# Seven block products instead of eight in two of eight weight pieces, in half of u and in z, with the scan's decay in another buffer

## The chip, the cores and the metric

One NeuronCore of a Trainium2 chip runs one program. The metric is the device time of one execution in microseconds, from runs of the unchanged kernel and of the changed one; lower is better. The engines are named as the profile names them: PE is TensorE's matmul side, PEld its weight loads, DVE is VectorE, ACT is ScalarE, POOL is GpSimd, SP is SyncE, which here only issues the weights' transfers.

## The reference

One decoder layer over 256 tokens of width 2048, float32, batch 1. The part that matters here is the mixer between two feed-forward blocks:

```
proj = rmsnorm(h, mix_norm) @ w_in            # 2048 x 10272
gu, gv, z, xbc, dt_raw = split(proj)          # u, v, z: 2048 columns each
a_out = chunked_sgu(gelu(gu), gelu(gv), ...)  # u * (W_s RMSNorm(v) + b)
...
seg   = cum[:, :, :, None] - cum[:, :, None]
decay = exp(where(causal, seg, -inf))         # 128 x 128 for each of 32 heads, in 2 chunks
y_diag = einsum('bclsg,bclsgr,bcsgrp->bclgrp', scores, decay, xdt)
...
m_out = rmsnorm(y * silu(z), ssm_norm)
h = h + concat([a_out, m_out]) @ w_out
```

## The kernel before

**Products.** Every float32 operand is split into a high part and the rest (`hi`, `lo`), and a product of two is three matmuls: hi by hi, hi by lo, lo by hi. Weights stream in pieces of 256 rows by 1024 columns (1 MB); a piece is the block matrix of 2 row blocks by 2 column groups of 512. ACT writes `hi` (`high`, L161), DVE writes `lo` (`split_op`, L169). There are three buffers for `raw`, three for `hi` and two for `lo`, so `lo` of a piece is written when the last piece but one is done.

**Two ways through a piece.** With 256 tokens as 2 blocks of 128, a piece is 8 block products of 128 x 128 by 128 x 512, so 24 matmuls. `proj_tok` (L204) does that: its operands are transposed tokens, four accumulators of 512 columns. `proj_sum` (L245) knows two kinds of pieces. A piece "C" is done plainly, 24 matmuls. A piece "S" is done with 7 block products, 21 matmuls, after Strassen and Winograd: DVE forms four sums of the weight blocks (`split_sums`, L189), these are split too (`wshigh`, `wslow`, one buffer each), and the token operand holds sums as well (`Pieces.sums`, L415). Four of the seven products lie in accumulators of their own (m1, m6, m5, m7), from which ACT and DVE build parts (`parts_of`, L468), to which the plain accumulators are added at the end. The feed-forward blocks, `w_out`, the values and `w_o` use `proj_sum` already; V, u and z, two halves each, use `proj_tok`.

**The scan.** `scan_start(t, j)` (L750) handles 16 heads of chunk t: it brings a row of 2048 cumulative sums from DRAM to all 128 partitions (tile `dec`, 1 MB, issued by POOL), and for j = 0 makes `xdt` and y times D. DVE then makes three passes over `dec` (minus `cum`, minimum with `lim`, and, after ACT's exponential, times the scores). `scan_apply` (L774) uses `dec` as weights for 16 matmuls in two accumulators (`yp`), which DVE adds to y. `dec` is a tile of the pool `big`, which has 12 buffers of 8 KB per partition and holds the operands too.

**What sets the order.** PE runs in program order, written by hand: `step()` counts half pieces and pieces, and `later(fn, by)` puts side work (transposes, the scan) at a step. The scan's four starts stand at steps 3, 7, 13, 17 from the start of V and its four applications at 7, 10, 17, 21 (L826). On DVE, ACT and POOL a scheduler orders the instructions when the program is built, and each engine runs its own in that order; waits are semaphores. `split_op` keeps the splits among themselves in order.

Of the kernel before, what the change touches and what calls it, by code (L numbers as in the profile page):

```python
# [46 lines left out]
def hybrid_layer(ctx: ExitStack, tc: tile.TileContext, x, mem, w_gu1, w_dn1, w_in, w_s, w_out,  # L47
# [24 lines left out]
    def matmul(out, lhsT, rhs, start=False, stop=False):  # L72
        return pe(nc.tensor.matmul(out, lhsT=lhsT, rhs=rhs, start=start, stop=stop))  # L73
# [130 lines left out]
    def proj_tok(w, r0, xts, cs, evac, kts=D // P):  # L204

        n = kts // KP
        ps = {}
        for i in range(n):
            hi, lo = split(load(w, r0 + i * KP * P, cs, PLAIN))
            order = [(t, k) for k in range(KP) for t in range(NT)]  # L210
            if i in (0, n - 1):
                order.sort()
            for t, k in order:
                if t not in ps:
                    ps[t] = [side("acc") for _ in range(2)]
# [109 lines left out]
        junk = half_k(F32, "junk")  # L325
        return nc.scalar.activation(junk, src, AF.Square, accum_out=ss)

    def rstd_of(ss, name):
        n = ss.shape[1]
        r = small.tile([P, n], F32, name=f"rstd_{name}", bufs=1)  # L330
# [107 lines left out]
    class Normed:  # L438


        def __init__(self, name, c0, kinds=None):
            self.name, self.c0 = name, c0
            self.xts = [] if kinds is None else Pieces(kinds, f"xp_{name}")
            self.ss = small.tile([P, NT, 4], F32, name=f"ss_{name}", bufs=1)

        def chunk(self, n, by=1):
            srcs = [h[n][:, t, :] for t in range(NT)]
            if isinstance(self.xts, Pieces):

                for i in (2 * n, 2 * n + 1):  # L450
                    later(lambda i=i: self.xts.put(i, srcs, i % 2 * KP, self.c0 + n * KG),
                          {4: 1, 6: 1.5, 5: 2.5, 7: 3}.get(i, by))
                later(lambda: self.stats(n), 3)
            else:
                operand_later(srcs, self.xts, f"xt_{self.name}{n}", self.c0 + n * KG, by)
                self.stats(n)

        def stats(self, n):
            for t in range(NT):
                sum_sq(self.ss[:, t, n:n + 1], h[n][:, t, :])  # L460
            if n == 3:
                self.rstd = rstd_of(self.ss, self.name)

    def axpy(y, a, x):
        return nc.vector.scalar_tensor_tensor(out=y, in0=x, scalar=a, in1=y, op0=ALU.mult, op1=ALU.add)
# [46 lines left out]
    def ffn(nrm, w_gu, w_dn, done=None, each=None, fine=0):  # L515
        for c_from, c_to in ((0, 5), (5, 11)):
# [61 lines left out]
    nx = Normed("mix", C_MIX)  # L578
    ffn(n1, w_gu1, w_dn1, nx.chunk, fine=2)


# [51 lines left out]
    def raw_dts():  # L633


        wd = whigh.tile([P, 2 * KP, NC], F32R, name="hi").rearrange("p a n -> p (a n)")[:, :2 * NC]
        wd = wd.rearrange("p (k h) -> p k h", h=2 * HEADS)
        nc.scalar.copy(out=wd[:, :, :HEADS], in_=raw_dt)
        nc.vector.tensor_tensor(out=wd[:, :, HEADS:], in0=raw_dt, in1=wd[:, :, :HEADS].bitcast(F32), op=ALU.subtract)
        pdt = side("dt")  # L640
        for k in range(D // P):
            matmul(pdt[:2 * HEADS, :], wd[:, k, :], nx.xts[k // KG][:, k % KG, :],
                   start=(k == 0), stop=(k == D // P - 1))
# [106 lines left out]
    def scan_start(t, j):  # L750
        hs = slice(j * 16, j * 16 + 16)
        if j == 0:
            scan["xdt"] = scan[f"xdt{t}"] = xdt = slot([P, HEADS, HD], F32, "xdt")
            nc.vector.tensor_tensor(out=xdt, in0=y[t], in1=per_head(dt[:, t, :], HD), op=ALU.mult)
            nc.vector.tensor_tensor(out=y[t], in0=y[t], in1=per_head(rowb[:, 2, :], HD), op=ALU.mult)
        dec = slot([P, 16, P], F32, "dec")
        nc.gpsimd.dma_start(
            out=dec.rearrange("p h l -> p (h l)"),
            in_=cum_rows[t:t + 1, j * 16 * P:(j + 1) * 16 * P].broadcast_to([P, 16 * P]))
# [101 lines left out]
    for c in (0, 2):  # L861
        gss = [[], []]

        def evac(t, ps):
            for j in range(2):
                g = half_k(F32, "gate")
                nc.scalar.activation(g, ps[j], AF.Gelu_apprx_tanh, scale=rstd[:, t:t + 1])
                nc.vector.scalar_tensor_tensor(out=g, in0=v[t][:, c + j, :],
                                               scalar=col[:, C_GB + c + j:C_GB + c + j + 1],
                                               in1=g, op0=ALU.add, op1=ALU.mult)  # L870
                gss[j].append(g)

        proj_tok(w_in, 0, nx.xts, (U0 + c * NC, U0 + (c + 1) * NC), evac)
        for j in range(2):
            ats.later(gss[j], by=1 + j)

    ss_m = small.tile([P, NT, 4], F32, name="ss_m", bufs=1)
    for c in (0, 2):
        def evac(t, ps):
            for j in range(2):  # L880
                g = half_k(F32, "gate")
                nc.scalar.activation(g, ps[j], AF.Silu, scale=rstd[:, t:t + 1])
                ys = y[t][:, (c + j) * 8:(c + j + 1) * 8, :].rearrange("p h d -> p (h d)")
                nc.vector.tensor_tensor(out=ys, in0=ys, in1=g, op=ALU.mult)
                sum_sq(ss_m[:, t, c + j:c + j + 1], ys)
# [112 lines left out]
    for hd in (0, 2):  # L998
# [106 lines left out]
```

## Time and profile before

| what | us |
|---|---|
| three runs, median (lowest to highest) | 2479.86 (2479.16 to 2480.48) |
| the profiled execution, its own time | 2480.06 |
| its span, first to last instruction | 2478.4 |
| PE busy in the span | 2461.7 |
| DVE busy | 1972.4 |
| ACT busy | 1287.9 |

Matmuls overlap at their ends, so PE's busy time counts a matmul of 512 columns with its latency; its pace is read from the distance between starts. A time in a row counts from the span's start.

### The profile page before, as it was taken

What the parts mean: (1) busy time and instruction counts of PE and PEld (TensorE: products, weight loads), DVE (VectorE), ACT (ScalarE), POOL (GpSimd) and SP (SyncE); (2) the same over time, 40 slices, a digit from 0 to 9 for tenths busy, and PEclk for the clock granted to TensorE, in tenths of its full rate; (3) what the DMA queues carried; (4) which work ended last, traced back from release to release, by engine and by line L of the source; (5) the groups of instructions that cost most, each with busy time, mean ns of one, the idle gap of its engine ahead of it and who ended that gap; (6) DMA issues with size and microseconds to landing.
All of it is one profiled execution on the core that took longest, in us unless ns stands there. A gap on an engine that the chain in (4) does not pass through costs nothing.

```text
span 2478.4 us, 31511 instructions
## 1 busy us (share of the span) xinstructions
PE 2461.7 (99%) x12673; PEld 2105.0 (85%) x12673; DVE 1972.4 (80%) x1834; ACT 1287.9 (52%) x1164; POOL 20.5 (1%) x46
## 2 busy tenths in 40 slices
PE   9999999999999999999999999999999999999998
PEld 7888888888899998788888999988888888888886
DVE  7999889999876668655698755678889988899987
ACT  6555445555545455435555544445555544555554
POOL 0000000000000000000000000000000000000000
PEclk9999999999999999999999999999999999999999
DMA  7565665665654555545566654555565656656664
GB/s 242 197 210 188 204 203 188 203 203 192 201 189 162 179 192 188 202 160 189 185 197 203 217 176 158 169 183 180 180 201 189 212 194 203 200 191 204 204 206 151
DMA packets 205763, 476.76 MB, mean 192 GB/s; under 512 B 15040, under 2 KB 17248, under 8 KB 204848
## 3 DMA queue, kind: packets, MB, share of 16 engines
q1 hardware_dynamic: 202800, 464.31, 57.3%
q0 software_dynamic: 1840, 9.26, 1.1%
q8 instruction: 99, 1.62, 0.3%
q10 hardware_dynamic: 976, 1.18, 0.1%
q14 instruction: 48, 0.39, 0.0%
HBM read 472.57 MB, written 2.13 MB: 192 GB/s over the span
## 4 chain that ended last, share of the span: by engine, by line
PE 96%; DVE 2%; ACT 1%; DMA 1%; issue 1%; POOL 0%; POOLq 0%; ACTq 0%; DVEq 0%; SPq 0%
PE acc L73 92%; PE tpose L76 2%; DVE lo L169 1%; PE yp L73 1%; PE logits L73 0%; PE o L73 0%; ACT hi L161 0%; DVE cacc L625 0%; DMA raw<-in_w_gu 0%; PE mixed L73 0%; PE dt L73 0%; DMA col<-in_cols 0%; PE scores L73 0%; DVE sum L169 0%; PE yo L73 0%
## 5 line engine op out<-in xcount | busy, mean ns | idle before, releaser
L161 ACT CAST hi<-raw 128x2048 fp32r<-128x2048 f32 (+1 forms) x438 | 791.6, 1807 | 838.3 <-PE acc L73 712.9
L169 DVE TENSOR_TENSOR lo<-raw,hi 128x2048 fp32r<-128x2048 f32 (+2 forms) x446 | 949.3, 2129 | 284.9 <-PE acc L73 224.9
L73 PE MATMUL acc<-hi,xp_ffn 128*128 128x512 f32 x1824 | 580.5, 391 | 0.9 <-ACT hi L183 0.9
L73 PEld LDWEIGHTS acc<-hi,xp_ffn 128*128 128x128 f32 x1824 | 342.4, 188 | 71.6 <-ACT hi L183 1.3
L73 PE MATMUL acc<-lo,xp_ffn 128*128 128x512 f32 x912 | 355.3, 390 | 1.9 <-DVE lo L169 1.9
L169 DVE TENSOR_TENSOR lo<-sum,hi 128x2048 fp32r<-128x2048 f32 x109 | 249.9, 2292 | 55.3 <-ACT hi L161 55.3
L73 PE MATMUL acc<-hi,hid 128*128 128x512 f32 x896 | 282.6, 390 | 0.0
L161 ACT CAST hi<-sum 128x2048 fp32r<-128x2048 f32 x109 | 208.8, 1916 | 105.4 <-DVE sum L169 85.6
L73 PE MATMUL acc<-hi,xt_mix 128*128 128x512 f32 x768 | 241.7, 393 | 0.0
L73 PEld LDWEIGHTS acc<-lo,xp_ffn 128*128 128x128 f32 x912 | 171.3, 188 | 37.5 <-DVE lo L169 2.9
L73 PEld LDWEIGHTS acc<-hi,hid 128*128 128x128 f32 x896 | 168.2, 188 | 34.7
L73 PE MATMUL acc<-xt_mix,hi 128*128 128x256 f32 x1024 | 186.0, 284 | 0.0
L504 DVE TENSOR_TENSOR part<-acc,part 128x512 f32<-128x512 f32 x240 | 159.0, 686 | 20.2 <-ACT part L471 7.8
L73 PE MATMUL acc<-lo,hid 128*128 128x512 f32 x448 | 174.6, 390 | 0.0
L73 PEld LDWEIGHTS acc<-hi,xt_mix 128*128 128x128 f32 x768 | 144.2, 188 | 30.3 <-issue 0.5
L73 PEld LDWEIGHTS acc<-xt_mix,hi 128*128 128x128 f32 x1024 | 159.6, 192 | 0.3
L169 DVE TENSOR_TENSOR sum<-sum,raw 128x512 f32<-128x512 f32 x218 | 150.7, 691 | 6.2
L73 PE MATMUL acc<-lo,xt_mix 128*128 128x512 f32 x384 | 149.6, 390 | 0.0
L73 PE MATMUL acc<-hi,xp_ffn1s 128*128 128x512 f32 x466 | 148.5, 389 | 0.0
L73 PE MATMUL acc<-hi,xp_ffn2s 128*128 128x512 f32 x466 | 148.5, 389 | 0.0
L73 PE MATMUL acc<-xt_mix,lo 128*128 128x256 f32 x512 | 145.2, 284 | 0.7 <-DVE lo L169 0.7
L169 DVE TENSOR_TENSOR sum<-raw 128x1024 f32<-128x1024 f32 x109 | 132.8, 1218 | 0.0
(282 smaller groups left out, 3371.1 us busy)
## 6 DMA issues: line engine op xcount, KB each, us to landing
raw<-in_w_gu SPq DMA_DIRECT2D x286, 512.0 KB, 3.9
raw<-in_w_in SPq DMA_DIRECT2D x80, 1024.0 KB, 5.1
raw<-in_w_dn SPq DMA_DIRECT2D x60, 1024.0 KB, 5.3
raw<-in_w_gu SPq DMA_DIRECT2D x132, 256.0 KB, 4.1
raw<-in_w_kv SPq DMA_DIRECT2D x28, 1024.0 KB, 5.3
raw<-in_w_out SPq DMA_DIRECT2D x21, 1024.0 KB, 5.5
raw<-in_w_q SPq DMA_DIRECT2D x16, 1024.0 KB, 5.2
raw<-in_w_dn SPq DMA_DIRECT2D x28, 512.0 KB, 4.0
```

The source lines that it names most:

```text
L73: return pe(nc.tensor.matmul(out, lhsT=lhsT, rhs=rhs, start=start, stop=stop))
L76: return pe(nc.tensor.transpose(out=out, in_=in_, identity=identity))
L161: nc.scalar.copy(out=t[:, :n], in_=x[:, :n])
L169: last_split[:] = [nc.vector.tensor_tensor(**kw).ins]
L504: nc.vector.tensor_tensor(out=out, in0=a, in1=b, op=op)
```

## The change

Four things change. The token operand of the mixer becomes pieces of the kinds "CCCSCSCC" in place of four plain tiles (`nx`, made at the end of the first feed-forward block); its last four pieces come at steps 1, 1, 2, 2 and the sums of squares for its norm at step 3, where they stood at the block's end. All its readers take the plain blocks out of either kind (`tokens`). The second half of u and both halves of z go through `column_pair`, so `proj_sum`, with pieces 3 and 5 of eight as S. The gates work in place on the parts. And `dec` becomes a tile of the pool `wshigh`, which has one buffer (it is named `hi` there), where it had its turn among the 12 of `big`; the operand now takes five of these where it took four.

```diff
+    MIX_KINDS = "CCCSCSCC"
+    nx = Normed("mix", C_MIX, MIX_KINDS, {4: 1, 5: 1, 6: 2, 7: 2})
...
-        dec = slot([P, 16, P], F32, "dec")
+        dec = wshigh.tile([P, 16, P], F32, name="hi")
         nc.gpsimd.dma_start(
             out=dec.rearrange("p h l -> p (h l)"),
...
+    def column_pair(w, xps, kinds, order, c, take):
+        parts = {}
+
+        def mid(banks):
+            parts.update(enumerate(parts_of(banks)))
+
+        def evac(t, j, ps):
+            x = parts[2 * t + j]
+            total(x, ps, x, ALU.subtract if (t, j) == (1, 0) else ALU.add)
+            take(j, t, x)
+
+        proj_sum(w, 0, xps, kinds, (c, c + NC), mid, evac, order)
...
+        if c == 0:
+
+            proj_tok(w_in, 0, nx.xts, (U0 + c * NC, U0 + (c + 1) * NC), evac)
+        else:
+            column_pair(w_in, nx.xts, MIX_KINDS, None, U0 + c * NC, lambda j, t, x: gate(j, t, x, x))
...
-        proj_tok(w_in, 0, nx.xts, (Z0 + c * NC, Z0 + (c + 1) * NC), evac)
+        column_pair(w_in, nx.xts, MIX_KINDS, None, Z0 + c * NC, take)
```

On POOL, in the first half of V, these stand in a row before (names: `wsr` is the gate's weights, `dec` the decay, `cum_rows` the sums in DRAM, `wn` a row of the gate's norm; in brackets the semaphores waited for, DMASW those of POOL's transfers):

```order
L813 DMA wsr<-in_w_s 128x4x128 [waits Activation_49]
L820 AFFINE_SELECT sum<-sum 128x512 [waits Activation_49]
L757 DMA dec<-cum_rows 128x2048 [waits DMASW1_49]
L757 DMA dec<-cum_rows 128x2048 [waits PE_49]
L757 DMA dec<-cum_rows 128x2048 [waits DMASW2_49,DVE_49,PE_49]
L334 TENSOR_TENSOR rstd_v<-ms,neghalf 128x2 [waits DVE_49]
```

And these with the change:

```order
L833 DMA wsr<-in_w_s 128x4x128 [waits Activation_49]
L840 AFFINE_SELECT sum<-sum 128x512 [waits Activation_49]
L777 DMA hi<-cum_rows 128x2048 [waits DMASW1_49,DVE_49,Pool_49]
L777 DMA hi<-cum_rows 128x2048 [waits DMASW4_49,DVE_49,PE_49]
L777 DMA hi<-cum_rows 128x2048 [waits DMASW2_49,DMASW5_49,DVE_49,PE_49]
L333 TENSOR_TENSOR rstd_v<-ms,neghalf 128x2 [waits DVE_49]
```

The order is the same; the second decay's PE wait was for a matmul of the feed-forward block long done, and is now for the last of the 16 `yp` matmuls of the first decay.

On DVE, at the scan's first start, these stand in a row before (with buffer numbers: `dec_7545` and `dec_7697` are the first and the second decay, `lo_7621` the rest of V's sixth piece, `lo_7651` that of the seventh):

```order
L169 TENSOR_TENSOR lo_7591<-raw_7587,hi_7589 128x2048
L732 COPY y0_6385<-tpose_7535 128x256
L754 TENSOR_TENSOR xdt_7542<-y0_6385,dt_5266 128x2048
L755 TENSOR_TENSOR y0_6385<-y0_6385,rowb_101 128x2048
L169 TENSOR_TENSOR lo_7621<-raw_7617,hi_7619 128x2048
L761 TENSOR_TENSOR dend_7421<-dec_7545,cum_5267 128x16
L762 TENSOR_TENSOR dec_7545<-dec_7545,cum_5267 128x2048
L761 TENSOR_TENSOR dend_7421<-dec_7697,cum_5267 128x16
L763 TENSOR_TENSOR dec_7545<-dec_7545,sum_5253 128x2048
L169 TENSOR_TENSOR lo_7651<-raw_7647,hi_7649 128x2048
L762 TENSOR_TENSOR dec_7697<-dec_7697,cum_5267 128x2048
```

And these with the change (`hi_7560` is the first decay, `lo_7636` the rest of the sixth piece, `lo_7666` that of the seventh):

```order
L169 TENSOR_TENSOR lo_7606<-raw_7602,hi_7604 128x2048
L781 TENSOR_TENSOR dend_7436<-hi_7560,cum_5263 128x16
L782 TENSOR_TENSOR hi_7560<-hi_7560,cum_5263 128x2048
L774 TENSOR_TENSOR xdt_7557<-y0_6400,dt_5262 128x2048
L783 TENSOR_TENSOR hi_7560<-hi_7560,sum_5249 128x2048
L775 TENSOR_TENSOR y0_6400<-y0_6400,rowb_101 128x2048
L169 TENSOR_TENSOR lo_7636<-raw_7632,hi_7634 128x2048
L790 TENSOR_TENSOR hi_7560<-hi_7560,scores_7566 128x2048
L169 TENSOR_TENSOR lo_7666<-raw_7662,hi_7664 128x2048
```

The sixth piece's `lo` has moved from ahead of the first read of the decay to behind it and behind four whole passes.

On DVE, at the scan's first application, these stand in a row before (`yp` are the accumulators of the first decay, `dec_7697` the second decay, two passes of which are done by then):

```order
L169 TENSOR_TENSOR lo_7713<-raw_7709,hi_7711 128x2048
L782 TENSOR_TENSOR y0_6385<-yp_7677,y0_6385 128x512
L782 TENSOR_TENSOR y0_6385<-yp_7687,y0_6385 128x512
L770 TENSOR_TENSOR dec_7697<-dec_7697,scores_7703 128x2048
L169 TENSOR_TENSOR lo_7755<-raw_7751,hi_7753 128x2048
```

And these with the change (`hi_7712` is the second decay, `lo_7804` the rest of the third piece of V's second half, `lo_7856` that of the fourth):

```order
L802 TENSOR_TENSOR y0_6400<-yp_7692,y0_6400 128x512
L802 TENSOR_TENSOR y0_6400<-yp_7702,y0_6400 128x512
L781 TENSOR_TENSOR dend_7436<-hi_7712,cum_5263 128x16
L782 TENSOR_TENSOR hi_7712<-hi_7712,cum_5263 128x2048
L169 TENSOR_TENSOR lo_7804<-raw_7800,hi_7802 128x2048
L783 TENSOR_TENSOR hi_7712<-hi_7712,sum_5249 128x2048
L169 TENSOR_TENSOR lo_7856<-raw_7852,hi_7854 128x2048
L790 TENSOR_TENSOR hi_7712<-hi_7712,scores_7718 128x2048
```

All passes over the second decay now stand behind the additions of the first one's results, with two `lo` between them.

## Rows read from the trace of the kernel before

**Rows 1.** The page, parts 1 and 4: busy time of each engine with its share of the span and its instructions; shares of the chain that ended last, by engine.

```profile
PE 2461.7 (99%) x12673; PEld 2105.0 (85%) x12673; DVE 1972.4 (80%) x1834; ACT 1287.9 (52%) x1164; POOL 20.5 (1%) x46
PE 96%; DVE 2%; ACT 1%; DMA 1%; issue 1%; POOL 0%; POOLq 0%; ACTq 0%; DVEq 0%; SPq 0%
```

**Rows 2.** The waits of PE, whole span: who waited for whom, us in total, times, the longest.

```profile
PE acc L73 <- DVE lo L169: 3.9, 9, 0.7
PE idle L73 <- DVE idle L564: 1.3, 1, 1.3
```

**Rows 3.** The page, part 5: the matmuls of V, u and z by their moving operand (two groups, 1152 in all: six halves of eight pieces of 24).

```profile
L73 PE MATMUL acc<-hi,xt_mix 128*128 128x512 f32 x768 | 241.7, 393 | 0.0
...
L73 PE MATMUL acc<-lo,xt_mix 128*128 128x512 f32 x384 | 149.6, 390 | 0.0
```

**Rows 4.** The timeline of PE in z: start, us, and the count of instructions merged.

```profile
1169.95 0.39 PE L73 MATMUL acc<-lo,xt_mix 128*128 128x512 f32 x1
1170.18 0.84 PE L73 MATMUL acc<-hi,xt_mix 128*128 128x512 f32 x3
1170.86 0.39 PE L73 MATMUL acc<-lo,xt_mix 128*128 128x512 f32 x1
1171.09 0.39 PE L73 MATMUL acc<-hi,xt_mix 128*128 128x512 f32 x1
1171.31 0.39 PE L73 MATMUL acc<-lo,xt_mix 128*128 128x512 f32 x1
```

**Rows 5.** The windows view, a stretch of the first feed-forward block and z: the stretch, its length, then busy us of PE, PEld, DVE, ACT and POOL, the granted clock, DMA share and GB/s.

```profile
100.00:200.00 100.00, 100.00 (x455) 83.10 (x454) 93.38 (x88) 57.30 (x46) 0.00 (x0) 1.00 0.59 193
...
1118.00:1208.00 90.00, 90.00 (x407) 74.70 (x406) 47.64 (x36) 44.44 (x42) 0.00 (x0) 1.00 0.58 188
```

**Rows 6.** The timeline of DVE in the first half of V, from the split of the fifth piece to the additions of the first `yp`; in brackets the idle time before and its releaser.

```profile
928.89 2.29 DVE L169 TENSOR_TENSOR lo<-raw,hi 128x2048 fp32r<-128x2048 f32 x1 [2.60 <-PE acc L73]
...
936.16 2.29 DVE L169 TENSOR_TENSOR lo<-raw,hi 128x2048 fp32r<-128x2048 f32 x1
938.36 0.18 DVE L761 TENSOR_TENSOR dend<-dec,cum 128x16 f32<-128x16 f32 x1
938.57 2.29 DVE L762 TENSOR_TENSOR dec<-dec,cum 128x2048 f32<-128x2048 f32 x1
...
945.31 2.28 DVE L762 TENSOR_TENSOR dec<-dec,cum 128x2048 f32<-128x2048 f32 x1
947.51 2.28 DVE L770 TENSOR_TENSOR dec<-dec,scores 128x2048 f32<-128x2048 f32 x1
949.71 2.28 DVE L763 TENSOR_TENSOR dec<-dec,sum 128x2048 f32<-128x2048 f32 x1
...
955.95 0.69 DVE L782 TENSOR_TENSOR y<-yp,y 128x512 f32<-128x512 f32 x1 [1.09 <-PE yp L73]
```

**Rows 7.** The timeline of POOL: issues of the decay's transfers (the first row holds two, the second of which was issued at 927.30).

```profile
926.75 1.09 POOL L757 DMA_DIRECT2D dec<-cum_rows  x2
991.45 0.53 POOL L757 DMA_DIRECT2D dec<-cum_rows  x1 [63.60 <-PE st L73]
...
1023.09 0.53 POOL L757 DMA_DIRECT2D dec<-cum_rows  x1 [3.09 <-PE yp L73]
```

**Rows 8.** The instructions of the tile `dec`: the four transfers from issue to landing, and DVE's wait for one.

```profile
DMA dec<-cum_rows: 6.8, 1
...
DMA to landing us min/median/max: 6.9/7.1/9.6
```

**Rows 9.** The timeline of DVE where it waits for the same `yp` as POOL's last issue of the decay.

```profile
1022.82 0.69 DVE L782 TENSOR_TENSOR y<-yp,y 128x512 f32<-128x512 f32 x1 [1.02 <-PE yp L73]
```

**Rows 10.** The timeline of PE in V: the first use of the sixth piece's `lo`, the first `yp` matmuls, the first use of the `lo` of the third piece of V's second half, and the `yp` matmuls of the second decay.

```profile
941.58 0.39 PE L73 MATMUL acc<-lo,xt_mix 128*128 128x512 f32 x1
...
952.24 0.55 PE L73 MATMUL yp<-xdt,dec 128*128 128x64 f32 x4
...
967.82 0.39 PE L73 MATMUL acc<-lo,xt_mix 128*128 128x512 f32 x1
...
973.04 3.68 PE L73 MATMUL yp<-xdt,dec 128*128 128x64 f32 x32
```

**Rows 11.** The timeline of ACT: the first decay's exponential.

```profile
943.37 1.91 ACT L764 ACTIVATE dec<-dec 128x2048 f32<-128x2048 f32 x1
```

**Rows 12.** The page, part 5: DVE's additional work for a piece S, and the additions of parts, with counts, busy us and mean ns.

```profile
L169 DVE TENSOR_TENSOR lo<-sum,hi 128x2048 fp32r<-128x2048 f32 x109 | 249.9, 2292 | 55.3 <-ACT hi L161 55.3
...
L504 DVE TENSOR_TENSOR part<-acc,part 128x512 f32<-128x512 f32 x240 | 159.0, 686 | 20.2 <-ACT part L471 7.8
...
L169 DVE TENSOR_TENSOR sum<-sum,raw 128x512 f32<-128x512 f32 x218 | 150.7, 691 | 6.2
...
L169 DVE TENSOR_TENSOR sum<-raw 128x1024 f32<-128x1024 f32 x109 | 132.8, 1218 | 0.0
```

**Rows 13.** Groups of instructions by shape, DVE, from 1100 to 1180 us: the gate's products and the operands `at`, `ats` made of u.

```profile
L868 DVE SCALAR_TENSOR_TENSOR gate<-v,col,gate 128x512 f32<-128x512 f32 x4 | 2.8, 748 | 1.3 <-ACT gate L867 1.3
...
L430 DVE TENSOR_TENSOR ats<-forms,ats 128x512 fp32r<-128x512 f32 x4 | 2.8, 688 | 0.2
...
L425 DVE TENSOR_TENSOR forms<-forms 128x256 f32<-128x256 f32 x2 | 0.9, 426 | 1.1 <-ACT forms L418 1.1
L426 DVE TENSOR_TENSOR forms<-forms 128x128 f32<-128x128 f32 x2 | 0.6, 291 | 0.1
```

**Rows 14.** The same view of PE: the transposes of u's products.

```profile
L76 PE MATMUL tpose<-ident,gate 128*128 128x128 f32 x16 | 2.1, 272 | 0.0
```

More of the change, by code (lines that the diff above doesn't have):

```diff
@@ L216, in proj_tok @@
                 kt = i * KP + k
-                xt = xts[kt // KG][:, kt % KG, :]
-                xh, xl = xt[:, t * P:(t + 1) * P], xt[:, S + t * P:S + (t + 1) * P]
+                xh, xl = tokens(xts[i], k, t)
                 first, last = kt == 0, kt == n * KP - 1
@@ L326, in sum_sq, with rstd_of @@
         return nc.scalar.activation(junk, src, AF.Square, accum_out=ss)
-    def rstd_of(ss, name):
+    def rstd_of(ss, name, r=None):
         n = ss.shape[1]
-        r = small.tile([P, n], F32, name=f"rstd_{name}", bufs=1)
+        r = small.tile([P, n], F32, name=f"rstd_{name}", bufs=1) if r is None else r
         ms = small.tile([P, n], F32, name="ms")
@@ L438, in hybrid_layer, with __init__ @@
     class Normed:
-        def __init__(self, name, c0, kinds=None):
+        def __init__(self, name, c0, kinds=None, bys=None):
+            self.bys = bys
             self.name, self.c0 = name, c0
@@ L444, in __init__ @@
             self.ss = small.tile([P, NT, 4], F32, name=f"ss_{name}", bufs=1)
+            self.rstd = small.tile([P, NT], F32, name=f"rstd_{name}", bufs=1)
         def chunk(self, n, by=1):
@@ L451, in chunk @@
                     later(lambda i=i: self.xts.put(i, srcs, i % 2 * KP, self.c0 + n * KG),
-                          {4: 1, 6: 1.5, 5: 2.5, 7: 3}.get(i, by))
+                          self.bys.get(i, by))
                 later(lambda: self.stats(n), 3)
@@ L461, in stats @@
             if n == 3:
-                self.rstd = rstd_of(self.ss, self.name)
+                rstd_of(self.ss, self.name, self.rstd)
     def axpy(y, a, x):
@@ L543, in ffn @@
             add_sum(w_dn, c_from * NC, hts, (kinds, kinds), turn, 0.5, done if last else None, each if last else None)
+    BYS = {4: 1, 6: 1.5, 5: 2.5, 7: 3}
     n1 = Normed("ffn1", C_FFN1, GU_KINDS)
@@ L577, in hybrid_layer @@
         later(lambda n=n: n1.stats(n), by=4 + n / 2)
-    nx = Normed("mix", C_MIX)
+    MIX_KINDS = "CCCSCSCC"
+    nx = Normed("mix", C_MIX, MIX_KINDS, {4: 1, 5: 1, 6: 2, 7: 2})
     ffn(n1, w_gu1, w_dn1, nx.chunk, fine=2)
@@ L641, in raw_dts @@
         for k in range(D // P):
-            matmul(pdt[:2 * HEADS, :], wd[:, k, :], nx.xts[k // KG][:, k % KG, :],
+            x, i = nx.xts[k // KP], k % KP
+            x = x[:, :, 2 * i:2 * i + 2].rearrange("p h f s -> p h (f s)") if len(x.shape) == 4 else \
+                x[:, i].rearrange("p (h s) -> p h s", h=2)
+            matmul(pdt[:2 * HEADS, :].rearrange("p (h s) -> p h s", h=2), wd[:, k, :], x,
                    start=(k == 0), stop=(k == D // P - 1))
@@ L862, in hybrid_layer, with gate @@
         gss = [[], []]
+        def gate(j, t, g, x):
+            nc.scalar.activation(g, x, AF.Gelu_apprx_tanh, scale=rstd[:, t:t + 1])
+            nc.vector.scalar_tensor_tensor(out=g, in0=v[t][:, c + j, :],
+                                           scalar=col[:, C_GB + c + j:C_GB + c + j + 1],
+                                           in1=g, op0=ALU.add, op1=ALU.mult)
+            gss[j].append(g)
         def evac(t, ps):
             for j in range(2):
[L866 to L873, printed above, removed]
+                gate(j, t, half_k(F32, "gate"), ps[j])
+        if c == 0:
+            proj_tok(w_in, 0, nx.xts, (U0 + c * NC, U0 + (c + 1) * NC), evac)
+        else:
+            column_pair(w_in, nx.xts, MIX_KINDS, None, U0 + c * NC, lambda j, t, x: gate(j, t, x, x))
         for j in range(2):
@@ L878, in hybrid_layer, with take @@
     for c in (0, 2):
[L879 to L885, printed above, removed]
-        proj_tok(w_in, 0, nx.xts, (Z0 + c * NC, Z0 + (c + 1) * NC), evac)
+        def take(j, t, g):
+            nc.scalar.activation(g, g, AF.Silu, scale=rstd[:, t:t + 1])
+            ys = y[t][:, (c + j) * 8:(c + j + 1) * 8, :].rearrange("p h d -> p (h d)")
+            nc.vector.tensor_tensor(out=ys, in0=ys, in1=g, op=ALU.mult)
+            sum_sq(ss_m[:, t, c + j:c + j + 1], ys)
+        column_pair(w_in, nx.xts, MIX_KINDS, None, Z0 + c * NC, take)
     rstd_m = rstd_of(ss_m, "m")
@@ L1016, in hybrid_layer @@
                 later(lambda hd=hd, j=j, q=q, vv=vvs[j]: weigh(hd + j, vv, q), by=1 + j)
-    n2 = Normed("ffn2", C_FFN2, GU_KINDS)
+    n2 = Normed("ffn2", C_FFN2, GU_KINDS, BYS)
     add_sum(w_o, 0, ots, (O_KINDS, O_KINDS), None, 1.0, n2.chunk)
```

## The prediction

> **What bounds the kernel now.** I read the page first: PE is busy for 99% of the span and holds 96% of the chain that ended last [rows 1]. Then the waits of PE: all that it waited for DVE's `lo` comes to 3.9 us in nine waits, none over 0.7 us, and the longest wait of any kind is 1.3 us [rows 2]. So the kernel's time is PE's matmuls laid end to end, each matmul less is worth its pace, and anything that makes PE wait is paid in full. The pace stands in the starts: from 1169.95 to 1171.31 us there are six matmuls of 512 columns, 0.227 us each [rows 4]. (The 390 ns in the groups are latency, which overlaps.) DVE has room in u and z: 47.6 of 90 us, against 93.4 of 100 in the feed-forward block, where the same mix of pieces already runs with PE at full pace [rows 5]. Last I went through DVE's own row of work in V, since the second part of the change touches a tile there.
>
> **Fewer matmuls.** V, u and z hold 1152 matmuls [rows 3]. An S piece has 7 products in place of 8, three matmuls each, so 3 less. Three halves with two S pieces make 18 less: 18 x 0.227 = 4.1 us saved, all on the path.
>
> **More work on DVE.** An S piece adds 1.22 + 2 x 0.69 us of sums and 2.29 us for their split, and saves a quarter of a `lo`; the parts add eight additions of 0.69 us for each half [rows 12]. For z's 90 us that is about 4 x 4.3 + 16 x 0.69 = 28 us on top of 47.6 [rows 5]: it fits as a sum. The narrow place is the start of z, where the operands made of u fall into the same stretch. From the end of u DVE has an addition and two gate products (2.2 us), two `lo` and another gate product (5.2), two operands of the sums kind and two plain ones (2 x 2.4 + 2 x 0.69 = 6.2), the sums (2.6), three quarters of a `lo` (1.7) and the sums' `lo` (2.3): 20.2 us [rows 6, 12, 13]. PE reaches that split after three pieces (16.3 us), sixteen transposes (2.1) and ten matmuls (2.3): 20.7 us [rows 4, 14]. That leaves next to nothing, so I allow 0.3 us of waiting there and in the next S piece, between 0 and 1.5. In u and in the second half of z no operands stand in the way, and I put them at 0. The operand's own forms at the end of the feed-forward block and the norm at step 3 stand on ACT and DVE in the shade of some 6 us of PE per step; I put them at 0 too, and at 1 us if the norm's chain comes late.
>
> **The decay's buffer, first wait.** Before, the first decay's transfer was issued at 926.75 us and a second one 0.55 us later [rows 7]; DVE had other work until 938.36 and waited for neither [rows 6]. With the change DVE's row is different: behind the fifth piece's split comes the first read of the decay at once, and the sixth piece's `lo` stands behind it and four passes of 128 x 2048. The earlier split ends at 931.18 [rows 6]. The transfers took 6.9 to 9.6 us from issue to landing, 7.1 in the median [rows 8]; I take 7.0, since the 9.6 is one of two in flight together. DVE then starts at 926.75 + 7.0 = 933.75; the short read takes 0.21 (938.36 to 938.57), the four passes 2.20 each (945.31, 947.51, 949.71), the `lo` 2.29 [rows 6]. It is there at 933.75 + 0.21 + 8.80 + 2.29 = 945.05. PE wants it at 941.58 [rows 10]; before it was there at 938.45 [rows 6]. PE waits 3.5 us, where it did not wait at all.
>
> **The decay's buffer, second wait.** The second decay has no buffer of its own any more: its transfer is issued when the last `yp` matmul of the first one is done. That was at 955.95, when DVE's waiting addition started [rows 6], and is 959.45 with the 3.5 us. Issue follows 0.27 us behind, as at 1022.82 and 1023.09 [rows 7, 9], landing 7.0 later, at 966.7. DVE has nothing left to do and waits, as it did for 6.8 us for the last decay of before [rows 8]. Then 0.21, a pass, a `lo`, a pass, a `lo` at 2.20 each, and the product with the scores, 2.28: 978.0. The exponential, 1.91 us on ACT [rows 11], lies behind the second `lo`. The first of these two `lo` ends at 971.4; PE wants it at 967.82 + 3.5 = 971.3 [rows 10]: even. The `yp` matmuls of the second decay want its product at 973.04 + 3.5 = 976.5 [rows 10]. PE waits another 1.5 us. From then on DVE has slack: the third decay is applied seven steps after the second, and the fourth waits as it did before.
>
> Both waits hang on the time from issue to landing, L: the first is L - 3.5, the second L - 5.5, together 2L - 9.0. That is 4.8 us at 6.9, 5.0 at 7.0, 5.2 at 7.1.
>
> The page "DMA: Bandwidth & Descriptors" of the Trainium skill (section "Anatomy of one DMA — SWDGE (gpsimd) path") fits 2.0 us plus bytes over 436e3 per us, an estimate of 4.4 us for this 1 MB; by it the decay would land before DVE is free, 0.9 us would remain of the first wait and nothing of the second, and the sum would be 2477.0. No transfer of this shape in the trace was under 6.9 us, so the sum goes by the row.
>
> **The sum,** against the profiled execution: 2480.06 - 4.1 + 5.0 + 0.3 = 2481.3. That execution lies 0.2 above the median of the three runs, so against the median it is 2481.1, 0.05% slower. A measurement of this kernel can tell about 0.2% from no change, 5.0 us: 2474.9 to 2484.8 counts as the same. The gain and the waits nearly cancel.
>
> **Rivals.**
> 1. *The waits don't come.* If the decay landed within 4.5 us of its issue, 0.9 us would be left of the first wait and nothing of the second: 2476.9; with no wait at all 2475.8. For it: one transfer in flight where there were two. Against it: no landing is under 6.9 us [rows 8], though the third and fourth transfers were issued singly [rows 7]. Chance 8%, a third of it below 2474.9.
> 2. *A slow landing; the change is slower.* One mechanism at the place above: the transfer takes as long as the slowest of before, 9.6 us [rows 8]. Then the waits are 2 x 9.6 - 9.0 = 10.2 us, and the time 2486.3. It decides for slower from L = 8.9 us on. For it: the weights' transfers go on beside it. Against it: the 9.6 belongs to a pair. Chance 7%.
> 3. *PE's clock falls in the gap.* The granted clock is 1.00 in both stretches of [rows 5], and no wait of before was over 1.3 us [rows 2]; the first wait here is 3.5 us long. If the clock went to the lower of its two levels, 1.2 for 2.4 GHz, a matmul would take 0.454 us until it comes back. No row shows that level, so the bounds are 0 and one piece, 24 x 0.227 = 5.4 us: 2481.1 to 2486.5. Chance 5%, half of it over 2484.8. The page "TensorE: Matmul & The Clock Gate" of the Trainium skill (section "HAM oscillation — how this bites in real kernels") warns of this for a PE that sits idle between bursts; no run here shows it so far.
>
> **How the numbers follow.** The forecast has 80%, with 2479 to 2483.5 from L of 6.8 to 7.6 us and the 0 to 1.5 us at the start of z; rival 1 has 8, rival 2 has 7, rival 3 has 5. The range of 8 in 10 reaches from 2477.0, which takes in most of rival 1, to 2484.5. Same: 80 + 5 + 2 = 87, I say 86; slower: 7 + 2.5, I say 10; faster: 4.
>
> **What would show it.** PE's waits on `lo` should hold one of some 3.5 us at the sixth piece of V's first half, and PE should wait for the decay's product in the `yp` matmuls some 1.5 us; DVE should show two waits for the transfer that it had not, 2.5 and 6.5 us. In u's second half and in z the groups of matmuls should count 12 and 6 less, at 0.227 us. If PE's waits in V are under 1 us, the second half of this argument is wrong, and the time is near 2476. If they are right and the time is still higher, the start of z or the mixer's start is where to look.

## The result, and the profile after

The changed kernel takes 2484.20 us in the median of 20 runs (2480.95 to 2487.27), the kernel before in the same comparison 2480.44 (20 runs, 2479.16 to 2482.24). The ratio is 1.0015, 95% interval 1.0010 to 1.0021: slower by 3.8 us, which is clear of the noise, inside the 0.2% that the prediction counted as the same, and inside its range, but 0.3 us from its upper end and 3.1 us over its point of 2481.1. The spread of the runs (highest less lowest) is also twice that of before, 6.3 us for 3.1. The profiled execution took 2483.6 us, its span is 2481.5, 3.1 longer than before.

The page of the changed kernel, part 1:

```profile
PE 2461.6 (99%) x12655; PEld 2104.4 (85%) x12655; DVE 2013.4 (81%) x1887; ACT 1299.5 (52%) x1178; POOL 20.6 (1%) x46
```

There are 18 matmuls less (12,673 before), and PE is just as busy. Groups of the matmuls of V, u and z by shape, against [rows 3]:

```profile
L73 PE MATMUL acc<-hi,xp_mix 128*128 128x512 f32 x576 | 182.7, 392 | 0.0
...
L73 PE MATMUL acc<-lo,xp_mix 128*128 128x512 f32 x288 | 112.3, 390 | 0.0
...
L73 PE MATMUL acc<-hi,xp_mixs 128*128 128x512 f32 x180 | 59.4, 401 | 0.0
...
L73 PE MATMUL acc<-lo,xp_mixs 128*128 128x512 f32 x90 | 36.0, 400 | 4.0 <-DVE lo L169 4.0
```

The `hi` groups count 756 and the `lo` groups 378: 12 and 6 less. The last row also holds the first of the two new waits. The waits of PE, against [rows 2] (us in total, times, longest):

```profile
PE acc L73 <- DVE lo L169: 6.3, 9, 4.0
...
PE yp L73 <- DVE hi L790: 1.1, 1, 1.1
```

One wait of 4.0 us for a `lo` and one of 1.1 for the decay's product are new. The rows of POOL that issue the first two decays, and DVE's timeline behind each, against [rows 6, 7]:

```profile
926.42 0.56 POOL L777 DMA_DIRECT2D hi<-cum_rows  x1
961.69 0.55 POOL L777 DMA_DIRECT2D hi<-cum_rows  x1 [34.71 <-PE yp L73]
```

```profile
933.92 0.18 DVE L781 TENSOR_TENSOR dend<-hi,cum 128x16 f32<-128x16 f32 x1 [3.15 <-DMA hi<-cum_rows]
934.14 2.29 DVE L782 TENSOR_TENSOR hi<-hi,cum 128x2048 f32<-128x2048 f32 x1
936.35 2.28 DVE L774 TENSOR_TENSOR xdt<-y,dt 128x2048 f32<-128x2048 f32 x1
938.55 2.28 DVE L783 TENSOR_TENSOR hi<-hi,sum 128x2048 f32<-128x2048 f32 x1
940.75 2.28 DVE L775 TENSOR_TENSOR y<-y,rowb 128x2048 f32<-128x2048 f32 x1
942.96 2.28 DVE L169 TENSOR_TENSOR lo<-raw,hi 128x2048 fp32r<-128x2048 f32 x1
...
968.65 0.18 DVE L781 TENSOR_TENSOR dend<-hi,cum 128x16 f32<-128x16 f32 x1 [6.53 <-DMA hi<-cum_rows]
...
977.68 2.28 DVE L790 TENSOR_TENSOR hi<-hi,scores 128x2048 f32<-128x2048 f32 x1
```

DVE waits 3.15 and 6.53 us for the transfers (from issue to first read 7.50 and 6.96 us). Behind the first of them the four passes run, and only then the `lo` that PE wants. PE's timeline there, against [rows 10] (each `yp` matmul shows as two records, so 16 of them are x32; the first `yp` row counts 13, because the stretch that was read ends there):

```profile
940.95 0.39 PE L73 MATMUL acc<-hi,xp_mixs 128*128 128x512 f32 x1
945.29 0.50 PE L73 MATMUL acc<-lo,xp_mixs 128*128 128x512 f32 x1 [3.96 <-DVE lo L169]
...
947.63 0.63 PE L73 MATMUL acc<-lo,xp_mixs 128*128 128x512 f32 x1
948.06 0.63 PE L73 MATMUL acc<-hi,xp_mixs 128*128 128x512 f32 x1
948.49 0.63 PE L73 MATMUL acc<-lo,xp_mixs 128*128 128x512 f32 x1
...
957.72 1.56 PE L73 MATMUL yp<-xdt,hi 128*128 128x64 f32 x13
...
980.02 3.79 PE L73 MATMUL yp<-xdt,hi 128*128 128x64 f32 x32 [1.05 <-DVE hi L790]
```

Read these starts against those of before. The `lo` of the sixth piece is used 3.7 us later (945.29 for 941.58), the first `yp` 5.5 later (957.72 for 952.24), the second `yp` 7.0 later (980.02 for 973.04), and the span ends 3.1 later. So 3.7 are lost by the first wait (4.0 of waiting, less some 0.3 by which this execution came earlier to that place), 1.8 right behind it, 1.5 by the second wait, and 3.9 are won behind it, where u and z lie. The 1.8 behind the first wait is PE's clock: the three starts from 947.63 are 0.43 us apart, not 0.227. The windows view shows the granted clock (the column before the DMA share):

```profile
944.80:945.79 0.99, 0.50 (x2) 0.45 (x3) 0.99 (x2) 0.00 (x0) 0.00 (x0) 1.00 0.00 0
945.79:949.20 3.41, 3.41 (x10) 2.66 (x9) 3.41 (x2) 0.00 (x0) 0.00 (x0) 0.50 0.78 252
949.20:950.20 1.00, 1.00 (x5) 0.80 (x5) 0.44 (x1) 0.00 (x0) 0.00 (x0) 1.00 0.49 197
```

PE runs at the lower level, 1.2 GHz, for 3.41 us. At 0.43 us for one, that is 8 matmuls where 15 would have run: 1.6 us. Before, the granted clock is 1.00 in V, u and z, and 0.50 only at the end: PE's last matmul starts at 2468.05 us, and from 2472 us on the lower level is granted, with no matmul left to slow down.

In z DVE is busy for 74.4 of 90 us, 26.8 more than before (the prediction had 28), and no wait of PE is recorded from 985 to 1260 us, which holds u and z:

```profile
1118.00:1208.00 90.00, 90.00 (x406) 74.44 (x405) 74.40 (x71) 50.82 (x48) 0.00 (x0) 1.00 0.61 197
```

### The profile page after: what moved, and what is told of

The parts are those of the page before. It is cut to its first block, busy times and chain, and to the rows that moved or that the text cites. A ratio compares the mean times of both kernels' runs of the same rounds, so it can differ in the third digit from the quotient of the medians.

```text
span 2481.5 us, 31561 instructions
## 1 busy us (share of the span) xinstructions
PE 2461.6 (99%) x12655; PEld 2104.4 (85%) x12655; DVE 2013.4 (81%) x1887; ACT 1299.5 (52%) x1178; POOL 20.6 (1%) x46
## 4 chain that ended last, share of the span: by engine, by line
PE 95%; DVE 2%; DMA 1%; ACT 1%; issue 1%; POOL 0%; POOLq 0%; SPq 0%; DVEq 0%; ACTq 0%
PE acc L73 91%; PE tpose L76 2%; DVE lo L169 1%; PE yp L73 1%; PE logits L73 0%; PE o L73 0%; DVE cacc L642 0%; DMA raw<-in_w_gu 0%; DMA hi<-cum_rows 0%; ACT hi L161 0%; PE mixed L73 0%; PE dt L73 0%; DMA h<-in_x 0%; DVE sum L169 0%; PE yo L73 0%
## 5 line engine op out<-in xcount | busy, mean ns | idle before, releaser
L169 DVE TENSOR_TENSOR lo<-sum,hi 128x2048 fp32r<-128x2048 f32 x115 | 263.6, 2292 | 57.0 <-ACT hi L161 57.0
L161 ACT CAST hi<-sum 128x2048 fp32r<-128x2048 f32 x115 | 220.3, 1916 | 117.0 <-DVE sum L169 97.7
L505 DVE TENSOR_TENSOR part<-acc,part 128x512 f32<-128x512 f32 x264 | 175.1, 686 | 22.2 <-ACT part L472 8.7
L73 PE MATMUL acc<-hi,xp_mix 128*128 128x512 f32 x576 | 182.7, 392 | 0.0
L169 DVE TENSOR_TENSOR sum<-sum,raw 128x512 f32<-128x512 f32 x230 | 158.9, 691 | 6.6
L73 PE MATMUL acc<-xp_mix,hi 128*128 128x256 f32 x768 | 140.1, 284 | 0.0
L73 PEld LDWEIGHTS acc<-hi,xp_mix 128*128 128x128 f32 x576 | 108.2, 188 | 22.6 <-issue 0.5
L73 PE MATMUL acc<-hi,hids 128*128 128x512 f32 x392 | 125.3, 389 | 0.0
L73 PEld LDWEIGHTS acc<-xp_mix,hi 128*128 128x128 f32 x768 | 119.7, 192 | 0.3
L73 PE MATMUL acc<-lo,xp_mix 128*128 128x512 f32 x288 | 112.3, 390 | 0.0
```

The source lines that it names most:

```text
L161: nc.scalar.copy(out=t[:, :n], in_=x[:, :n])
L169: last_split[:] = [nc.vector.tensor_tensor(**kw).ins]
```

## The experiments

The theory after the result: -4.1 us of matmuls, +5.1 of two waits that hang on the decay's single buffer, and some 2 to 3 us in the median for the clock behind a wait. The rivals: the waits come from the seven-product pieces; the clock falls whatever PE waits for; the matmuls bring less than their pace. The runs of before beside these had medians of 2480.34 and 2480.53.

**The decay's buffer alone.**

```diff
--- the kernel before
-        dec = slot([P, 16, P], F32, "dec")
+        dec = wshigh.tile([P, 16, P], F32, name="hi")
```

> The kernel before with one edit: the decay is a tile of the sums' buffer; all pieces of u and z stay plain, so all 24 matmuls of each are there. Theory (the change is three terms: -4.1 us of matmuls, +5.1 us of two waits through the single buffer, +2 to 3 us of lower clock behind the first wait): the waits of 4.0 and about 1.1 us and the clock's fall are here too, at the same places, and the gain is not: 2484.2 + 4.1 = 2488.3 us, 7 to 8 us over the kernel before, in a spread of some 6 us. Rival A (the waits come from the seven-product pieces and their load on DVE, not from the buffer): 2480.4. Rival B (the 18 matmuls bring less than their pace, because the kernel's end does not follow PE): under 2487, nearer to 2484.

Measured: 2493.20 us (2492.83 to 2495.71, 5 runs), ratio 1.0055 (1.0043 to 1.0068). Rival A falls: the buffer alone costs 12.9 us, without one seven-product piece in u or z. That is 5 more than expected, and its trace shows where. Its waits of PE, and the granted clock in the two stretches where it fell:

```profile
PE acc L73 <- DVE lo L169: 7.1, 10, 3.5
PE yp L73 <- DVE hi L770: 3.3, 1, 3.3
```

```profile
944.89:948.30 3.41, 2.86 (x7) 2.28 (x8) 3.41 (x3) 0.00 (x0) 0.00 (x0) 0.50 0.49 125
...
982.44:992.68 10.24, 10.24 (x41) 9.46 (x41) 6.17 (x5) 0.00 (x0) 0.53 (x1) 0.50 0.70 246
```

The second wait is 3.3 us here, since `xdt` of the next chunk stands among DVE's passes ahead of the product (an order that this kernel has and the changed one has not), and the clock falls at both waits, for 3.41 and for 10.24 us. At 0.43 for 0.227 us the second fall costs 4.8, an estimate. Because of this other order the run does not measure what the 18 matmuls bring: rival B is left to the run with both waits taken away.

**The first wait taken away.** DVE's reads of the first decay stand behind the sixth piece's `lo`; transfer and buffer are as in the changed kernel (issued at 926.21 us; the four landings of this trace took 7.0 to 7.3 us).

```diff
--- the changed kernel, scan_start
+        if (t, j) == (0, 0):
+            later(lambda: scan_work(t, j, dec, sc), by=3)
+        else:
+            scan_work(t, j, dec, sc)
+
+    def scan_work(t, j, dec, sc):
+        with behind(last_split if t == 0 else ()):
...
```

> The changed kernel with DVE's three passes over the first decay put behind the sixth piece's rest in V's first half; its transfer is issued where it was, and the buffer stays single. Theory: the 4.0 us wait for that rest goes, and with it the fall of the clock (no gap of 4 us is left ahead of it); the 1.1 us wait of the second decay stays, since its transfer still waits for the first decay's last matmul. 2484.2 - 4.0 - 2.8 = 2477.4 us, spread of the runs under 4 us. Rival A (the clock falls for another reason, such as the length of the run): the wait goes and the fall stays, 2480.2 with a spread of 6 us. Rival B (the passes come too late for the product with the decay instead): a wait of 1 to 3 us at the first yp matmuls, 2479 to 2481.

Measured: 2478.00 us (2476.76 to 2480.89, 11 runs), ratio 0.9991 (0.9982 to 1.0000). Its waits:

```profile
PE acc L73 <- DVE lo L169: 2.7, 9, 0.5
...
PE yp L73 <- DVE hi L799: 1.1, 1, 1.1
```

The 4.0 us are gone, the 1.1 stay, and its profile has no fall of the clock in V, so rivals A and B are out for this execution. The median is 0.6 above what was expected and the spread, 4.1 us, not under 4. 6.2 us are won for a wait of 4.0: the rest fits the clock, of which the changed kernel's trace showed 1.6 to 1.8. Two of its eleven runs, at 2480.6 and 2480.9, have a mean clock of 0.997, the nine others 0.998 or 0.999; this is taken up below.

**Both waits taken away.** Besides, the second decay lies where it need not wait for the first.

```diff
--- the kernel of the last experiment
-        room, name = (wshigh, "hi")
+        room, name = ((wslow, "lo") if (t, j) == (0, 1) else (wshigh, "hi"))
         dec = room.tile([P, 16, P], F32, name=name)
```

> The same order of DVE's row as in the run before it, and the second decay lies in the buffer of the sums' rest, which is free until the states are made, so that its transfer does not wait for the first decay's matmuls. Theory: no wait over 1 us in V is left, and only the 18 matmuls are saved: 2480.4 - 4.1 = 2476.3 us, 1.1 under the run before it, clock 0.999 in all runs. Rival (a cost of the seven-product pieces at u and z that the two waits hid): 2477.5 to 2478.5 with a new wait at the start of z or of u's second half.

Measured: 2476.53 us (2475.47 to 2478.08, 11 runs), ratio 0.9985 (0.9976 to 0.9994). This version beats both kernels: 3.8 us under before in the same comparison, where 18 x 0.227 = 4.1 were expected, and all its runs are at 0.998 or 0.999. So the 18 matmuls bring nearly their pace, and rival B of the first experiment falls here, with this one's own rival. The longest wait for a `lo` that is left is 0.9 us:

```profile
PE acc L73 <- DVE lo L169: 3.6, 10, 0.9
```

**PE kept busy in the first wait.** Seven matmuls of zeros (two records each, x14 below) stand where PE waits for the sixth piece's `lo`; nobody reads their sums.

```diff
--- the changed kernel, proj_tok for the first half of V
                     matmul(ps[t][j], xh, hi[:, 2 * k + j], start=first)
+                    if fill and (i, t, k, j) == (5, 0, 0, 0):
+                        keep_busy(fill)
```

> The changed kernel with seven matmuls of zeros (128x128 by 128x256, some 3.0 us together by the estimate of 0.43 us each, two thirds of the 634 ns that the same ones took at the program's start) put behind the first matmul of the sixth piece of V's first half, where PE waits 4.0 us for the piece's rest; they go to an accumulator that nobody reads. Theory: DVE's row and both waits' ends stay, PE waits under 1.2 us instead of 4.0 in one stretch, and the clock does not fall: 2484.2 - 2.8 = 2481.4 us, spread of the runs under 4 us. Rival A (the fall does not hang on the gap): 2484.2 with the same spread. Rival B (the zeros are slower than 0.57 us each and push the piece back): over 2484.2.

Measured: 2482.28 us (2480.34 to 2485.13, 11 runs), ratio 1.0010 (1.0000 to 1.0019). PE's timeline:

```profile
941.17 3.18 PE L73 MATMUL idle<-idle 128*128 128x256 f32 x14
945.27 0.50 PE L73 MATMUL acc<-lo,xp_mixs 128*128 128x512 f32 x1 [0.91 <-DVE lo L169]
```

The `lo` is used at 945.27, as in the changed kernel, and the profile has no fall of the clock: in this execution (2481.77 us) rival A is out, with 1.8 us less than the profile of the changed kernel. But the median is 0.9 above what was expected, and the spread, 4.8 us, is not under 4. Something varies from run to run that the first wait doesn't explain. Theory 2 for that: the second wait makes the clock fall too, in some runs. Theory 1: the falls belong to the first wait, or to what is left of it. Four kernels with the first wait whole or filled, the second whole, filled or taken away:

```diff
--- the second decay's room, in the changed kernel
+        room, name = (wslow, "lo") if (t, j) == (0, 1) else (wshigh, "hi")
+        with behind(last_split if (t, j) == (0, 1) else ()):
...
--- two more matmuls of zeros, scan_apply
+            if (t, j, q) == (0, 1, 0):
+                keep_busy(2)
```

> The changed kernel with the second decay in the buffer of the sums' rest; DVE's row at the first decay is as in the changed kernel, so the first wait of 4.0 us stays and the second (1.1 us) goes. Theory 1 (the clock falls behind the first wait): 2484.2 - 1.1 = 2483.1 us, runs still spread over 5 us or more, a fall of the clock at the sixth piece in the profile. Theory 2 (the falls that vary from run to run belong to the second wait, whose 16 matmuls of 64 columns follow it): 2481.5 us, spread under 3 us.

> The second decay in the buffer of the sums' rest, and seven matmuls of zeros (3.2 us measured) in the first wait. Of the first wait 0.9 us in one stretch stays, the second is gone. In the run with the zeros alone 5 of 11 runs lay at 2483.1 or above at a clock of 0.997 to 0.999. Theory 2 (those falls belong to the second wait): 2484.2 - 1.1 - 2.6 = 2480.5 us, spread under 3 us. Theory 1 (they belong to what is left of the first wait): 2482.3 - 1.1 = 2481.2 us with a spread of some 5 us.

> The changed kernel with seven matmuls of zeros in the first wait and two (0.9 us by the 3.2 us of seven) ahead of the second decay's yp matmuls, so that both waits end when they did, but PE stands still in neither. Theory 2 (the second wait makes the clock fall in some runs): 2484.2 - 2.6 = 2481.5 us, spread under 3 us. Theory 1 (the falls belong to what is left of the first wait, or to no wait): 2482.3 us with a spread of some 5 us, as with the first wait alone filled.

| first wait | second wait | median us (range), runs |
|---|---|---|
| whole | whole (the changed kernel) | 2484.20 (2480.95 to 2487.27), 20 |
| whole | taken away | 2483.01 (2481.74 to 2484.43), 11 |
| filled | whole | 2482.28 (2480.34 to 2485.13), 11 |
| filled | taken away | 2481.11 (2480.73 to 2482.04), 11 |
| filled | filled | 2481.30 (2480.30 to 2483.45), 11 |

The ratios to before of the second, fourth and fifth row are 1.0011 (1.0002 to 1.0020), 1.0003 (0.9994 to 1.0012) and 1.0003 (0.9994 to 1.0013). Neither theory is right alone. With the first wait whole and no second one, all eleven runs have a mean clock of 0.997 or 0.998 (in the fourth row, with this wait filled, 0.998 or 0.999), which fits a fall behind the first wait in each of them, and the profile shows one of 6.83 us:

```profile
943.55:950.38 6.83, 6.14 (x15) 4.84 (x15) 6.80 (x5) 0.23 (x1) 0.00 (x0) 0.50 0.59 169
```

So theory 1's median is right (2483.1) and its spread wrong. With the first wait filled, taking the second away takes the spread from 4.8 us to 1.3, as theory 2 has it; the median is theory 1's (2481.2), since this kernel has a new wait of 1.2 us for a `lo`, at 972.14, that theory 2's 2480.5 left out. With both filled the time is 2481.30 (theory 2: 2481.5), and the spread of 3.2 us is just over the 3 of theory 2, by one run at 2483.45. The two runs at 0.997 of the kernel without the first wait also fit a fall behind the second one. Filling both waits, which takes nothing from DVE's row or the transfers, gives back 2484.20 - 2481.30 = 2.9 us of the median. Not all of it need be the clock: in the two profiles, 2.3 us apart, the filled kernel's first decay landed 0.7 us sooner and its second 0.5 us later, and some 2 us are left for the clock.

**The fall behind the second wait, seen.** The kernel with the first wait filled, three more executions, to have the trace of one that falls:

> The kernel with zeros in the first wait once more, for a trace of an execution in which the clock falls: 5 of its 11 runs lay at 2483.1 us or above. Theory 2: if this one does, the lower level stands behind the second wait, from about 978 us of the span, and the time over 2481.5 us is half its length; behind the first wait (945 us) there is none. Theory 1: the lower level stands behind the 0.9 us that are left of the first wait.

> The same as the run before it, another execution: a fall of the clock, if there is one, behind the second wait (theory 2) or behind what is left of the first (theory 1).

> The same as the two runs before it, another execution: a fall of the clock, if there is one, behind the second wait (theory 2) or behind what is left of the first (theory 1).

Measured: 2483.10, 2484.16 and 2485.01 us, one execution each. The third shows a fall, the granted clock by windows:

```profile
979.08:980.08 1.00, 1.00 (x11) 1.00 (x11) 1.00 (x1) 0.06 (x1) 0.00 (x0) 1.00 0.96 393
980.08:986.91 6.83, 6.83 (x25) 6.06 (x25) 3.60 (x4) 0.00 (x0) 0.53 (x1) 0.50 0.79 267
```

It falls 2 us behind the end of the second wait (1.1 us, at 978.05) and not at 945 us. The two others have no fall; what they have more is waits for `lo`, 4.4 and 5.5 us in all where the first execution had 4.0, and they are 0.5 and 0.8 us late at the sixth piece's `lo` already (945.79 and 946.12 for 945.27). The rest is the second decay's landing. Issue and first read of it, in the execution profiled first (2481.77 us) and in these two:

```profile
960.04 0.55 POOL L779 DMA_DIRECT2D hi<-cum_rows  x1 [33.06 <-PE yp L73]
966.55 0.18 DVE L783 TENSOR_TENSOR dend<-hi,cum 128x16 f32<-128x16 f32 x1 [6.08 <-DMA hi<-cum_rows]
...
960.55 0.55 POOL L779 DMA_DIRECT2D hi<-cum_rows  x1 [32.98 <-PE yp L73]
968.04 0.18 DVE L783 TENSOR_TENSOR dend<-hi,cum 128x16 f32<-128x16 f32 x1 [7.06 <-DMA hi<-cum_rows]
...
960.92 0.55 POOL L779 DMA_DIRECT2D hi<-cum_rows  x1 [32.47 <-PE yp L73]
968.74 0.18 DVE L783 TENSOR_TENSOR dend<-hi,cum 128x16 f32<-128x16 f32 x1 [7.39 <-DMA hi<-cum_rows]
```

From issue to first read that is 6.51, 7.49 and 7.82 us, and the second `yp` starts at 977.91, 979.41 and 980.11: 1.5 and 2.2 us later than in the first, where the times are 1.3 and 2.4 us longer. So in this kernel the spread comes in part from the clock, and in part from the landing and from what came earlier in the program.

In the changed kernel itself the clock's part is the larger one: sorted by time, its 20 runs are sorted by mean clock too, 0.999 for the fastest (2480.95), 0.998 from 2481.32 to 2484.45, 0.997 from 2485.00 to 2486.19, 0.996 from 2486.58 to 2487.27. A mean clock lower by 0.001 is some 5 us more at the lower level, so some 2.3 us lost, an estimate from the two paces; three such steps make 7 us, for a spread of 6.3.

**The transfer issued earlier.** This was to test the formula by which the first wait is the landing less 3.5 us.

```diff
--- the changed kernel, gate_weights (the decay's transfer is issued ahead, at step 1)
-        nc.gpsimd.affine_select(out=wst, in_=wst, pattern=[[0, 4], [1, P]], compare_op=ALU.is_ge, fill=0.0,
...
+        with behind([scan["dma"]]):
+            nc.gpsimd.affine_select(out=wst, in_=wst, pattern=[[0, 4], [1, P]], compare_op=ALU.is_ge, fill=0.0,
...
+    later(lambda: scan_fetch(0, 0), by=1)
```

> The changed kernel with one row of POOL moved: the first decay's transfer is issued ahead of the gate's masking (which waits 8.5 us for ACT there), some 9 us earlier; DVE's, ACT's and PE's rows are in the same order. It tests the formula of the prediction, by which the first wait is the landing minus 3.5 us: DVE's wait of 3.15 us for the transfer goes, and of PE's 4.0 us there remain 0.8. With a clock that falls only behind the long wait: 2484.2 - 3.2 - 1.7 to 2.6 = 2478.4 to 2479.3 us. Rival A (PE waits for DVE's four passes whatever the landing): 2484.2. Rival B (the wait shrinks and the clock still falls): 2481.

Measured: 2485.01 us (2481.80 to 2489.22, 11 runs), ratio 1.0018 (1.0009 to 1.0027): no gain, and my expectation fails. The timeline of POOL and of DVE:

```profile
926.54 0.54 POOL L772 DMA_DIRECT2D hi<-cum_rows  x1 [9.29 <-ACT xf L644]
```

```profile
933.06 0.18 DVE L786 TENSOR_TENSOR dend<-hi,cum 128x16 f32<-128x16 f32 x1 [2.26 <-DMA hi<-cum_rows]
```

The transfer is first in POOL's row, and still issued at 926.54, so the edit did not do what it was made for, and the expectation's rivals stay untested. POOL's wait of 9.29 us is put down to the convolution (ACT, L644), whose padded inputs (`misc2`, L604) lie in the same buffer; DVE's last instructions that read them (L642) run until 925.9. The wait for the masking, which I had read from POOL's row, hid that one. So the buffer is in use on both sides of the first decay. The formula is tested all the same, since the landing differs from trace to trace. Issue, first read and PE's wait with the buffer alone, then with the second decay's room, and PE's wait with the transfer first in the row:

```profile
927.06 0.56 POOL L757 DMA_DIRECT2D hi<-cum_rows  x1
934.07 0.18 DVE L761 TENSOR_TENSOR dend<-hi,cum 128x16 f32<-128x16 f32 x1 [2.65 <-DMA hi<-cum_rows]
945.44 0.80 PE L73 MATMUL acc<-lo,xt_mix 128*128 128x512 f32 x1 [3.46 <-DVE lo L169]
...
926.18 0.55 POOL L778 DMA_DIRECT2D hi<-cum_rows  x1
932.87 0.18 DVE L783 TENSOR_TENSOR dend<-hi,cum 128x16 f32<-128x16 f32 x1 [2.34 <-DMA hi<-cum_rows]
944.24 0.80 PE L73 MATMUL acc<-lo,xp_mixs 128*128 128x512 f32 x1 [3.15 <-DVE lo L169]
...
944.43 0.50 PE L73 MATMUL acc<-lo,xp_mixs 128*128 128x512 f32 x1 [3.07 <-DVE lo L169]
```

| kernel | from issue to first read, us | less 3.5 | PE's first wait |
|---|---|---|---|
| changed kernel | 933.92 - 926.42 = 7.50 | 4.0 | 3.96 |
| buffer alone | 934.07 - 927.06 = 7.01 | 3.5 | 3.46 |
| second decay's room | 932.87 - 926.18 = 6.69 | 3.2 | 3.15 |
| transfer first in the row | 933.06 - 926.54 = 6.52 | 3.0 | 3.07 |

The prediction's second formula, landing less 5.5, can be read from the same traces, as what lies between the starts of the first and the second `yp` over the 20.80 us of before:

| kernel | from issue to first read, us | less 5.5 | first to second `yp`, over 20.80 |
|---|---|---|---|
| changed kernel | 6.96 | 1.5 | 1.50 |
| first wait filled, three executions | 6.51, 7.49, 7.82 | 1.0, 2.0, 2.3 | 1.05, 2.03, 2.36 |
| first wait taken away | 7.32 | 1.8 | 1.85 |
| transfer first in the row | 7.33 | 1.8 | 1.89 |

## Why the prediction was right, and what it mis-sized

**Fewer matmuls: right.** 12 and 6 less; 3.9 us won between the second `yp` and the end of the span, 3.8 in the median with both waits away, for 4.1.

**The first wait: right in place, cause and formula.** It was put at 3.5 us with a landing of 7.0; the landing was 7.50 in the profile, and the wait 3.96. The buffer causes it, not the pieces (it comes with the buffer alone), through DVE's order: with the `lo` ahead of the passes it is gone, with the transfer issued at the same place and landing in the same buffer. For this transfer the page "DMA: Bandwidth & Descriptors" of the Trainium skill (section "Anatomy of one DMA — SWDGE (gpsimd) path") gives the estimate of 4.4 us that the prediction quoted; in the ten traces in which DVE waits for the first decay it took 6.35 to 7.50 us from issue to first read, so the measurement decides against it here, and rival 1 did not come. That no landing is under 6.9, as rival 1 had it from the trace of before, does not hold in general: the second decay's transfer, issued at 787 us in the kernel with both waits taken away, landed in 4.9 us.

**The second wait: right, and its formula too.** 1.5 us were put; the second `yp` is another 1.5 us late, 1.05 of it recorded as a wait, and in the other traces the lateness follows the landing.

**The start of z: 0.3 us put, none found** (bounds 0 to 1.5). The feed-forward block that the prediction held against it does not run the same mix: three of eight pieces are S there (`GU_KINDS`), so it was the harder case.

**The clock: this is the term that was mis-sized.** The prediction saw that a wait of 3.5 us could bring PE to the lower level, put that at 5% as rival 3, and left 0 in the sum, because no row of before showed such a fall. With a chance of 5% that was far too low: in all four traces in which PE stood still for a first wait of 3.1 to 4.0 us, the clock fell. It is no rival but part of the likeliest case: 1.8 us in the profile, 2.9 in the median by whole against filled waits, if the landings were alike in these runs. The trace of before did hold the lower level, at its end behind PE's last matmul, and no row of it was read. With the clock's 1.8 us the sum is 2480.06 - 4.1 + 4.0 + 1.5 + 1.8 = 2483.3 for the profiled execution, which took 2483.6. The kernel with both waits filled, with the landings of its own trace (6.77 and 7.45 us, so waits of 3.3 and 1.9 by the two formulas), comes to 2480.44 - 4.1 + 5.2 = 2481.5, and took 2481.30. So waits and matmuls nearly cancel, as the prediction said (ratio 1.0003, no change within the noise), and the clock makes the change measurably slower. The page "TensorE: Matmul & The Clock Gate" of the Trainium skill (section "HAM oscillation — how this bites in real kernels") warns of a PE idle between bursts, and the traces agree: 0.50 granted behind waits of 3.1 to 4.0 us.

**That the number fell into the range is in part luck.** The forecast's own span ended at 2483.5, and 2484.20 lies above it; only the wider range, to 2484.5, takes it in, by 0.3 us. The lower end of that span, 2479, does not follow from its terms either: a landing of 6.8 us and no wait in z give 2480.4. Nor does the third of rival 1 below 2474.9, whose own prices are 2475.8 and 2476.9. And the last sign (waits right and the time still higher) pointed to the start of z or of the mixer; the time was lost right behind the first wait.

What stays open: why a wait of 1.1 us, ahead of `yp` matmuls of 64 columns, brings the fall in some executions and not in others of the same kernel (one was traced), what makes a fall 3.41, 6.83 or 10.24 us long, and why the landing differs from execution to execution. How the 2.9 us of the median divide between clock and landing is not shown.

## What to carry to other kernels

A tile that moves into a single buffer brings its transfer's landing into the order of the engine that reads it first: look at what stands behind that first read, and put what the bound engine wants ahead of it. On a PE at 99%, a new wait like those here, of 3.1 to 4.0 us, is to be costed with the clock behind it (here 1.6 to 4.8 us for one), not with its length alone. And before a transfer is moved ahead, all of its waits are to be read, not the one that came last.

## What was not expected of the hardware

At the lower level a matmul of 512 columns took 0.427 us (947.63, 948.06, 948.49), which is 512 columns at 1.2 GHz; the prediction had put twice 0.227. At the upper level the pace is 0.227 us, where 512 columns at 2.4 GHz would take 0.213 by the same reckoning, an estimate; so the fall costs a factor of 1.88 and not two. And the clock can fall before the wait is over: with the buffer alone at 944.89, 0.55 us ahead of the next matmul, and with the second decay's room at 943.55.
